# A two-layer decoder trunk: the first queries' PSUM banks emptied by ScalarE, the rotary work moved in the order, and new prices in the planner

## The chip, the cores and the metric

One Trainium2 chip, one of its eight cores. The metric is device time in microseconds of one execution. TensorE is called PE, VectorE DVE, ScalarE ACT, GpSimd POOL, and SyncE SP (here it only issues DMAs).

## The reference, cut to what matters

Two layers over 256 tokens of width 1024. Each normalises the residual stream, projects it, mixes tokens, gates the result, projects back and adds; then a gated projection of a side input is added. Layer 0 mixes by causal attention of 16 heads of 64 (with one block of 256 it is plain causal attention). Layer 1 mixes by three branches: compressed, selected and windowed keys.

```python
q = rope(rms_norm(split_heads(q, N_HEADS), q_gain), pos)   # likewise k; v is taken as it is
...
def compress(x, pe, w1, w2):
    idx = np.arange(nc)[:, None] * CMP_STRIDE + np.arange(CMP_LEN)[None, :]
    blocks = x[:, :, idx] + pe
    flat = blocks.reshape(B, G, nc, CMP_LEN * HEAD_DIM)
    return jax.nn.gelu(flat @ w1) @ w2
```

## The kernel before

**Projections.** A `Unit` is one 512-column slice of a projection. Its weights come in four groups (`step(g)`) of 128x1024 f32, 512 KB each. A group is loaded into one of five `raw` buffers by an SP DMA, rounded to fp32r by ACT (`hi<-raw`), and DVE takes the rest (`lo<-raw,hi`); the `raw` buffer is free again only when `lo` is done. The activations are split likewise (`ah`, `al`). A group then takes 12 matmuls of 512 columns: two 128-row tiles by two halves of the tokens by three products (`hi,ah`, `hi,al`, `lo,ah`). Matmuls into one bank keep their order, so a late `lo` stops all that follow on that bank. The result stands in two PSUM banks with the tag `mm`, of which there are four.

**Layer 0, first half of the heads** (`moba_half(0)`). The queries' unit `uq0` is read together with x itself; then come the keys' unit (groups called k0 to k3 here) and the values' (v0 to v3). `rope` takes the banks of the queries or the keys: ACT squares them into `tmp`, DVE sums the squares (`ssq`), makes `r` from them and from `e2`, POOL raises `r` to the power -1/2 (`r_q`, `r_k`, 128x16), and DVE multiplies the banks by the tables of cosines and sines times gain (`tq`, `tk`, made by `tables` from `cst` and `gmoba`), adds, and for keys multiplies by `r_k`. For queries DVE makes `nr_q` from `r_q`. PE then transposes `q` and `k` for the attention (`moba_attn`). After the values comes the queries' unit of the second half of the heads (uq1), which needs two of the four banks.

**Layer 1.** In `KC` the compressed branch's input `cc` is spread into windows with the position table added: 16 DVE `tensor_tensor` of 128x120 (`big<-big,pe`), whose source advances 16 elements at a time; `W(g)` multiplies the windows by the first compression weights.

**The order.** Nothing runs as it is written: `Plan.record` collects all operations, and `schedule` gives each engine a fixed order. It always takes the operation that can start first by its own prices, and of equals the one recorded first. So a step that is recorded earlier has the higher rank. Engines run their list in order, so an operation that the planner thought ready holds up everything behind it. The prices that matter: a power on POOL of n elements per partition is 900 + 130n ns (`cost`); a DMA moves 225 bytes/ns up to 6 us and 340 after (`RATE`, used in `schedule`); a DVE `tensor_tensor` is 65 + 1.04n ns. `hold` keeps DMAs back until a given operation has started: `gnsa`, `pe` and `w2`, which layer 1 needs, are held until the values' first load of the second half.

In `moba_half(0)` the recorded order is k0, k1, constants, norm, tables, rope of q, k2, k3, masks, rope of k, v0 to v3.

Of the kernel before, what the change touches and what calls it, by code (L numbers as in the profile page):

```python
# [7 lines left out]
F32 = mybir.dt.float32  # L8
F32R = mybir.dt.float32r
AF = mybir.ActivationFunctionType  # L10
OP = mybir.AluOpType
AX = mybir.AxisListType

P = 128
# [2 lines left out]
KT = 8  # L17
HD = 64
EPS = 1e-6
SWITCH = 150.0  # L20
NRAW, NHI, NLO, NPT, NA = 5, 5, 5, 9, 9
WARM = 15
ORDER = ("vw KE vs VS KT QE0 0A 0S1 0S0 VW 0T0 0S3 0T1 kc 0S2 1A 0T3 0T2 KC 1S0 1T0 q1.0 1S2 W0 q1.1 q1.2 1S3 "
         "0V 1T2 q1.3 W1 1S1 W2 1T3 W3 QE1 2A WE 2S2 0c 2S0 1c 1T1 1V 2T0 0b 2T2 2c 2S1 1b 2B 3A 3c 2T1 2S3 "
         "3S1 2T3 2V 3S0 3T1 3T0 3B 3S3 3S2 3T2 3T3 3V")

CST, CST_N = {}, 0
for _k, _n in (("ident", 128), ("cos", 128), ("sin", 128), ("mask", 384), ("cmask", 32), ("valid", 2), ("rmask", 4),
# [5 lines left out]
class View:  # L34
# [30 lines left out]
    def elems(self):  # L65
        n = 1
        for _, c in self.ap.ap[1:]:
            n *= c
        return n


class Tile_:
# [4 lines left out]
class Plan:  # L77
# [77 lines left out]
    def cost(self, op, views, first):  # L155
        n = first.elems() if isinstance(first, View) else 0
        e, m = op.engine, op.method
        if e == "sync":
            v = first if isinstance(first, View) else op.args[1]
            return v.elems() * 4 * v.ap.ap[0][1]  # L160
        if e == "tensor":
            k, c = op.args[1].ap.ap[0][1], op.args[1].ap.ap[1][1]
            op.mode = tuple(128 if x > 64 else 64 if x > 32 else 32 for x in (k, c))
            if m == "transpose":
                return 109.2
            if op.args[1].ap.dtype == mybir.dt.bfloat16:
                return 2.5 + n / 1.2
            if op.args[1].ap.dtype == F32R:
                return (n + 32) / 2.4 if n > 128 else 110

            return 2 * max(54.6 if op.mode == (128, 64) else 109.2, 2 * n / 2.4 / (2 if op.mode == (128, 64) else 1))
        if e == "gpsimd":
            if op.kwargs.get("op") == OP.pow:
                return 900 + 130.0 * n
            return 100 + 2.3 * n
        psum = any(self.tags[v.tile.tag]["psum"] for v in views)
        rows = first.ap.ap[0][1]
        half = 110 if rows in (60, 64) and (any(v.box()[0] != first.box()[0] for v in views)
                                            or psum and first.ap.dtype == F32R and e == "vector") else 0
        if e == "scalar":  # L180
            if m == "dma_start":
                return first.elems() * 4 * first.ap.ap[0][1]
            if first.tile.tag == "early":
                return 1500.0
            c = (60 if psum else 100) + 0.833 * max(n, op.args[1].elems())
            return half + c + 93 * sum(isinstance(op.kwargs.get(k), View) for k in ("scale", "bias", "accum_out"))
        if m == "tensor_tensor_reduce":
            return 130 + 1.04 * n
        if m == "reciprocal":
            return 65 + 6.9 * n  # L190
        if m == "tensor_reduce":
            return 65 + 1.04 * op.args[1].elems()
        two = len([v for v in views if v.elems() > 2 and v is not first]) > 1
        if not psum and not two and m in ("tensor_copy", "tensor_scalar"):
            return 70 + half + 0.52 * n + 60 * any(isinstance(x, View) and x.elems() == 1 for x in op.args[2:])
        return 65 + half + 1.04 * n + (65 if m == "scalar_tensor_tensor" and isinstance(op.args[2], View) else 0)

    LAT = {"PE": 200.0, "DVE": 140.0, "ACT": 160.0, "POOL": 200.0, "DMA": 100.0}
    START = {"PE": 110.0}

    ISSUE, LAG, RATE = 450.0, 2250.0, (225.0, 340.0)
    OWN = {"DVE": 127.0, "POOL": 127.0}

    def lat(self, a, b):
# [14 lines left out]
    def hold(self, since, i):  # L219

        for o in self.ops[since:]:
            o.after.append(i)

    def schedule(self):
        ops = self.ops
# [42 lines left out]
        while len(order) < n:  # L268
# [45 lines left out]
            by = "DMA" if o.method == "dma_start" else e  # L314
            if o.method == "dma_start":
                t = max(s + self.LAG, moved)
                moved = finish[i] = t + o.cost / self.RATE[t > 6000.0]
                free[e] = s + self.ISSUE
            else:
                finish[i] = free[e] = s + o.cost * (1.8 if e == "PE" and s < 5200.0 else 1.0)  # L320
# [54 lines left out]
def trunk(ctx: ExitStack, tc: tile.TileContext, a, out):  # L375
# [29 lines left out]
    def load_consts(lo, hi):  # L405
        nc.sync.dma_start(cst[:, lo:hi], a["cst"][:, lo:hi])

    def load_gains(t, lo, n):
        src = a["head_gain"]
        nc.sync.dma_start(t, bass.AP(tensor=src.tensor, offset=src.offset + 2 * HD * lo, ap=[[0, P], [1, 2 * HD * n]]))  # L410
# [159 lines left out]
            nc.copy(self.bc, ps[:, :T])  # L570


    def rope(ps, tab, nb, norm, is_q, tag, bufs):
        o = work.tile([P, 2, 512], F32, tag=tag, name=tag, bufs=bufs).rearrange("p t (h d) -> p t h d", d=HD)
        ssq = work.tile([P, 2, 8], F32, tag="ssq", name="ssq")
        for t in range(2):
            sq = tmp("hsq").rearrange("p (h d) -> p h d", d=HD)
# [28 lines left out]
    def evac_tok(o, ps, n, norm):  # L606
        for t in range(2):
            nc.scalar.activation(o[:, t], ps[t][:, :n], AF.Copy, scale=norm.rstd[:, t:t + 1])
# [116 lines left out]

    def moba_half(h):
        uq = Unit(a["moba_in"][1], False, x0).all() if h else uq0
        uk = Unit(a["moba_in"][2 + h], False, x0)
        early = 0 if h else 2
        loads = []  # L730
        for g in range(early):
            loads.append(len(nc.ops))
            uk.step(g)
        if h == 0:
            since = len(nc.ops)
            load_consts(0, 384)
            load_gains(gmoba, 0, 2)
            nc.hold(since, loads[1])

            for k in range(KT):  # L740
                n0.add(k)
            n0.finish()
            tab.append(tables("tq0", gmoba, [0]))
            tab.append(tables("tk0", gmoba, [1]))
        tq0, tk0 = tab
        q, nr = rope(uq.ps, tq0, 1, n0, True, "q", 2)
        for g in range(early, 4):
            loads.append(len(nc.ops))
            uk.step(g)
        if h == 0:  # L750
            since = len(nc.ops)
            load_consts(384, CST_N)
            nc.hold(since, loads[3])
        k, _ = rope(uk.ps, tk0, 1, n0, False, "k", 2)
        held_at.append(len(nc.ops))
        uv = Unit(a["moba_in"][4 + h], False, x0).all()
        v = work.tile([P, 2, 512], F32, tag="v", name="v")
        evac_tok(v, uv.ps, 512, n0)
        return q, nr, k, v

    def stack_moba(ps):

# [75 lines left out]
    g0 = out_proj(0, xo, n1)  # L838


    since = len(nc.ops)
    load_gains(gnsa, 2, 4)
    nc.hold(since, held_at[1])
    tq1 = tables("tq1", gnsa, [0])
    tk1 = tables("tk1", gnsa, [2, 3])
    nc.gpsimd.tensor_tensor(cosc, cosc, gnsa[:60, 1, 0], op=OP.mult)
    nc.gpsimd.tensor_tensor(sinc, sinc, gnsa[:60, 1, 1], op=OP.mult)
    since = len(nc.ops)
    pe = consts.tile([P, 2, 16], F32, name="pe")
    nc.sync.dma_start(pe, a["pe"])  # L850
    w2 = consts.tile([P, 2, 2, HD], F32, name="w2")
    nc.sync.dma_start(w2, a["w2"])
    nc.hold(since, held_at[1])


    n2 = Norm()
# [205 lines left out]
    def KC():  # L1062

        cc2 = big("cc").rearrange("p k t -> p (k t)")
        cc = [cc2[:, 0:1024], cc2[:, 1024:2048]]
        ukc = units["kc"]
        for i in range(2):
            cg = cc[i].rearrange("p (g t) -> p g t", g=4)
            cn = tmp("cn").rearrange("p (a b) -> p a b", a=2)
            nc.vector.tensor_tensor(cn, ukc.ps[i].rearrange("p (a b) -> p a b", a=2),  # L1070
                                    n2.bc[:, None, :].to_broadcast([P, 2, T]), op=OP.mult)
            for s in range(2):
                for d in range(2):

                    nc.copy(cg[d * HD:d * HD + HD, s::2, 0:T - d], cn[s * HD:s * HD + HD, :, d:T])
        kcB = consts.tile([P, 4, 32], F32, name="kcB")
        vcB = consts.tile([P, 16, HD], F32R, name="vcB")
        nc.gpsimd.memset(kcB, 0.0)
        win = []
        wins = big("win").rearrange("p k t -> p (k t)")  # L1080
        for i in range(2):
            w = wins[:, 960 * i:960 * i + 960].rearrange("p (t g n) -> p t g n", t=16, g=4)
            cg = cc[i].rearrange("p (g t) -> p g t", g=4)
            for h in range(2):
                for g in range(4):
                    src = cg[:, g, 16 * h:16 * h + 240].rearrange("p (n t u) -> p t n u", t=8, u=2)[:, :, :, 0]
                    nc.vector.tensor_tensor(w[:, 8 * h:8 * h + 8, g], src,
                                            pe[:, i, 8 * h:8 * h + 8, None].to_broadcast([P, 8, 15]), op=OP.add)
            win.append(w.rearrange("p t g n -> p t (g n)"))
        ST["win"], ST["B"], ST["y"] = win, (kcB, vcB), bank("mm", 4)  # L1090

# [201 lines left out]
```

## Time and profile before

| | us |
|---|---|
| median of 3 runs | 376.25 (375.98 to 376.69) |
| the profiled execution | 376.59 |
| its span in the trace | 374.5 |
| PE busy | 362.9 (97%) |
| DVE busy | 328.4 (88%) |
| ACT busy | 265.8 (71%) |
| POOL busy | 30.3 (8%) |

All times below are in us from the start of the span; 2.1 us of the execution lie outside it. A busy PE is not PE at its peak, since matmuls are pipelined and their ends are modelled: a matmul of 512 columns is shown as 0.39 us long, while the next one starts 0.23 us after it. In a timeline row the bracket gives the idle time of the engine just before the row, and who ended it; "x3" says that three instructions were merged into the row, and the time is then that of all.

### The profile page before, as it was taken

Reading aid. Unit: us, or ns where it says so; the run is one execution under the profiler, and the core shown is the slowest. Engines: PE = TensorE matmul, PEld = TensorE weight load, DVE = VectorE, ACT = ScalarE, POOL = GpSimd, SP = SyncE. Lnnn points to the kernel's source line nnn. Section 1 sums busy time; section 2 is a strip of 40 time slices with the busy share of each in tenths; the row PEclk is TensorE's granted clock in tenths of the full one; section 3 lists DMA queues with packets and bytes.
Section 4 is the critical chain, followed back from the end, with each engine's and each line's share of the span. In section 5 each row is a group of like instructions: output and inputs, shape, how many; then the busy total and the mean of one; then the engine's idle time right before and its main releaser. Section 6 shows DMA issues by size and latency. Waiting matters only on the chain.

```text
span 374.5 us, 7157 instructions
## 1 busy us (share of the span) xinstructions
PE 362.9 (97%) x2576; PEld 322.9 (86%) x2576; DVE 328.4 (88%) x820; ACT 265.8 (71%) x576; POOL 30.3 (8%) x21
## 2 busy tenths in 40 slices
PE   8989799999999999999999999999999999999994
PEld 6657687789999999999889999756997998999994
DVE  5877998999799895979979999998998999968864
ACT  6665478698789885755934979768966899947611
POOL 0017300330000000000013300000300000000000
PEclk9999999999999999999999999999999999999998
DMA  7976483333742445553454754054873200564012
GB/s 212 298 300 226 169 298 139 118 109 115 270 152 95 131 151 186 167 171 114 115 178 133 270 170 170 2 194 162 319 281 115 84 3 3 168 226 170 0 41 74
DMA packets 19907, 58.97 MB, mean 157 GB/s; under 512 B 2464, under 2 KB 5152, under 8 KB 19872
## 3 DMA queue, kind: packets, MB, share of 16 engines
q1 hardware_dynamic: 19584, 58.37, 45.7%
q8 instruction: 20, 0.33, 0.4%
q10 hardware_dynamic: 288, 0.15, 0.1%
q14 instruction: 15, 0.12, 0.1%
HBM read 57.46 MB, written 1.05 MB: 156 GB/s over the span
## 4 chain that ended last, share of the span: by engine, by line
PE 70%; DVE 21%; issue 4%; DMA 2%; POOL 2%; SPq 0%; ACT 0%; DVEq 0%; ACTq 0%
PE mm L353 53%; PE tr L353 10%; PE s L353 8%; DVE lo L353 4%; DVE sm L353 3%; DVE big L353 2%; DVE tmp L353 2%; POOL r_q L353 2%; DMA raw<-in_moba_in 2%; DVE k L353 1%; DVE q L353 1%; DVE ssq L353 1%; DMA gain_in<-in_gain_in 1%; DVE hl L353 1%; DVE pc L353 1%
## 5 line engine op out<-in xcount | busy, mean ns | idle before, releaser
L353 ACT ACTIVATE hi<-raw 128x1024 fp32r<-128x1024 f32 (+2 forms) x100 | 99.8, 1007 | 36.3 <-PE mm L353 16.2
L353 DVE TENSOR_TENSOR lo<-raw,hi 128x1024 fp32r<-128x1024 f32 (+2 forms) x100 | 114.2, 1156 | 5.7 <-ACT hi L353 5.3
L353 PE MATMUL mm<-ah,hi 128*128 128x256 f32 x416 | 118.6, 286 | 0.0
L353 PE MATMUL mm<-al,hi 128*128 128x256 f32 x416 | 118.4, 286 | 0.0
L353 PE MATMUL mm<-ah,lo 128*128 128x256 f32 x416 | 118.3, 286 | 0.0
L353 PEld LDWEIGHTS mm<-ah,hi 128*128 128x128 f32 x416 | 79.4, 191 | 0.8 <-issue 0.4
L353 PEld LDWEIGHTS mm<-al,hi 128*128 128x128 f32 x416 | 79.6, 192 | 0.4
L353 PEld LDWEIGHTS mm<-ah,lo 128*128 128x128 f32 x416 | 79.3, 191 | 0.5 <-issue 0.2
L353 PE MATMUL mm<-lo,ah 128*128 128x512 f32 (+2 forms) x178 | 67.7, 381 | 1.4 <-DVE lo L353 1.3
L353 PE MATMUL mm<-hi,ah 128*128 128x512 f32 (+2 forms) x178 | 67.0, 380 | 0.6 <-ACT hi L353 0.5
L353 PE MATMUL mm<-hi,al 128*128 128x512 f32 (+2 forms) x178 | 67.1, 377 | 0.0
L353 ACT ACTIVATE sm<-sm,nb 128x128 f32<-128x128 f32 (+1 forms) x96 | 42.8, 450 | 8.5 <-DVE nb L353 8.3
L353 PEld LDWEIGHTS mm<-lo,ah 128*128 128x128 f32 x178 | 34.0, 191 | 8.4 <-DVE lo L353 3.6
L353 PEld LDWEIGHTS mm<-hi,ah 128*128 128x128 f32 x178 | 33.8, 192 | 6.5 <-ACT hi L353 1.5
L353 PEld LDWEIGHTS mm<-hi,al 128*128 128x128 f32 x178 | 34.1, 192 | 5.4 <-DVE al L353 0.3
L353 DVE CUSTOM_DVE_ANT_0 sm<-s,cst,nr_q 128x128 f32<-128x128 f32 (+1 forms) x96 | 35.5, 411 | 0.3
L353 PE MATMUL tr<-cst,sm 128*128 128x128 f32 x144 | 24.8, 278 | 0.7 <-DVE sm L353 0.7
L353 ACT ACTIVATE pt<-tr 128x384 f32<-128x384 f32 x48 | 21.7, 482 | 4.8 <-PE tr L353 4.6
L353 POOL TENSOR_TENSOR r_q<-r,neg_half 128x16 f32<-128x16 f32 x5 | 18.0, 3599 | 44.0 <-DVE r L353 44.0
L353 PEld LDWEIGHTS tr<-cst,sm 128*128 128x128 f32 x144 | 17.1, 141 | 4.9 <-DVE sm L353 1.6
L353 ACT ACTIVATE tmp<-tmp 128x512 f32<-128x512 f32 (+2 forms) x21 | 11.1, 533 | 14.3 <-DVE tmp L353 14.2
L353 POOL TENSOR_TENSOR rstd<-ms,neg_half 128x2 f32<-128x2 f32 x4 | 4.0, 1006 | 209.8 <-DVE ms L353 209.8
(165 smaller groups left out, 543.6 us busy)
## 6 DMA issues: line engine op xcount, KB each, us to landing
raw<-in_moba_in SPq DMA_DIRECT2D x28, 512.0 KB, 4.6
raw<-in_nsa_in SPq DMA_DIRECT2D x24, 512.0 KB, 4.4
raw<-in_w_out SPq DMA_DIRECT2D x16, 512.0 KB, 4.5
raw<-in_ple_gate SPq DMA_DIRECT2D x16, 512.0 KB, 3.5
raw<-in_w SPq DMA_DIRECT2D x8, 512.0 KB, 3.6
raw<-in_ple_proj SPq DMA_DIRECT2D x4, 512.0 KB, 4.6
raw<-in_nsa_vs SPq DMA_DIRECT2D x4, 304.0 KB, 3.1
xT<-in_x SPq DMA_DIRECT2D x8, 128.0 KB, 4.9
```

Source lines behind the costliest of these rows:

```text
L353: getattr(getattr(self.nc, o.engine), o.method)(*[real(x) for x in o.args], **{k: real(x) for k, x in o.kwargs.items()})
```

## The change

It has four parts. In `moba_half(0)` the recorded order is now k0, k1, constants, norm, `qe`, k2, k3, masks, tables, v0, v1, rope of q, v2, v3, rope of k, evacuation of v; `qe` is new: two ACT copies of the queries' banks to SBUF, after which `rope` reads SBUF in place of PSUM. The second half keeps its order. The DMAs of `gnsa`, `pe` and `w2` are held only until v3's load of the first half. The position additions are 4 operations of 480 elements in place of 16 of 120. And the planner's prices change: a power 2300 + 130n ns, three DMA rates, a `tensor_tensor` with a wide source step 65 + 1.75n ns.

```diff
-SWITCH = 150.0
+SWITCH, POW = 150.0, 2300.0
...
+HALVES = ("k0 k1 consts norm qe k2 k3 masks tabs v0 v1 q v2 v3 k v", "q k0 k1 k2 k3 k v0 v1 v2 v3 v")
...
             if op.kwargs.get("op") == OP.pow:
-                return 900 + 130.0 * n
+                return POW + 130.0 * n
...
+        if m == "tensor_tensor" and args_step(op.args[1]) >= 16:
+            return 65 + 1.75 * n
...
-    ISSUE, LAG, RATE = 450.0, 2250.0, (225.0, 340.0)
+    ISSUE, LAG, RATE = 450.0, 2250.0, ((6000.0, 225.0), (26000.0, 280.0), (1e9, 340.0))
...
-                moved = finish[i] = t + o.cost / self.RATE[t > 6000.0]
+                moved = finish[i] = t + o.cost / next(r for end, r in self.RATE if t < end)
...
+    def rope_evac(ps, tag, bufs):
+
+        o = work.tile([P, 2, 512], F32, tag=tag, name=tag, bufs=bufs)
+        for t in range(2):
+            nc.scalar.activation(o[:, t], ps[t], AF.Copy)
+        return o
+
+    def rope(ps, tab, nb, norm, is_q, tag, bufs, o=None):
+        if o is None:
+            o = work.tile([P, 2, 512], F32, tag=tag, name=tag, bufs=bufs)
+        else:
+            ps = [o[:, t] for t in range(2)]
+        o = o.rearrange("p t (h d) -> p t h d", d=HD)
...
+        def qe():
+            o["q"] = rope_evac(uq.ps, "q", 2)
...
+        def q():
+            out["q"], out["nr"] = rope(uq.ps, tab[0], 1, n0, True, "q", 2, o.get("q"))
...
+        for step in HALVES[h].split():
+            if step in parts:
+                parts[step]()
+            else:
+                loads.append(len(nc.ops))
+                {"k": uk, "v": uv}[step[0]].step(int(step[1]))
         if h == 0:
-            since = len(nc.ops)
-            load_consts(384, CST_N)
-            nc.hold(since, loads[3])
...
+            held_at.extend(loads)
...
-    since = len(nc.ops)
-    load_gains(gnsa, 2, 4)
-    nc.hold(since, held_at[1])
+    nc.hold_on(lambda: load_gains(gnsa, 2, 4), held_at[7])
...
             for h in range(2):
-                for g in range(4):
-                    src = cg[:, g, 16 * h:16 * h + 240].rearrange("p (n t u) -> p t n u", t=8, u=2)[:, :, :, 0]
-                    nc.vector.tensor_tensor(w[:, 8 * h:8 * h + 8, g], src,
-                                            pe[:, i, 8 * h:8 * h + 8, None].to_broadcast([P, 8, 15]), op=OP.add)
+                src = cg[:, :, 16 * h:16 * h + 240].rearrange("p g (n t u) -> p t g n u", t=8, u=2)[:, :, :, :, 0]
+                nc.vector.tensor_tensor(w[:, 8 * h:8 * h + 8], src,
+                                        pe[:, i, 8 * h:8 * h + 8, None, None].to_broadcast([P, 8, 4, 15]), op=OP.add)
```

## Rows read from the trace of the kernel before

**Rows 1.** Stretches: busy (x instructions) of PE, weight loads, DVE, ACT, POOL; clock, DMA, GB/s.
```profile
18.00:25.00 7.00, 6.35 (x29) 4.67 (x29) 4.82 (x11) 4.15 (x5) 0.00 (x0) 1.00 1.00 380
25.00:36.00 11.00, 9.70 (x42) 7.18 (x42) 8.20 (x17) 6.43 (x8) 7.71 (x2) 1.00 0.58 194
36.00:47.00 11.00, 9.02 (x42) 7.06 (x41) 11.00 (x19) 5.50 (x7) 2.90 (x1) 1.00 0.50 175
47.00:57.00 10.00, 9.54 (x47) 7.66 (x45) 9.81 (x23) 7.37 (x16) 0.92 (x2) 1.00 0.88 299
57.00:70.00 13.00, 13.00 (x70) 10.61 (x71) 11.96 (x34) 10.43 (x22) 2.90 (x1) 1.00 0.23 82
...
225.00:245.00 20.00, 19.01 (x112) 15.62 (x112) 19.62 (x75) 15.33 (x49) 0.31 (x1) 1.00 0.23 80
```
**Rows 2.** Waits from 15 to 62 us: total, times, longest.
```profile
DVE nr_q L353 <- POOL r_q L353: 2.8, 1, 2.8
...
DVE tq L353 <- DMA gmoba<-in_head_gain: 2.2, 1, 2.2
...
PE tr L353 <- DVE k L353: 2.0, 2, 1.8
```
**Rows 3.** Timeline of PE: start, length, what, idle before.
```profile
22.10 0.50 PE L353 MATMUL mm<-lo,ah 128*128 128x512 f32 x1 [0.60 <-DVE lo L353]
...
28.22 0.49 PE L353 MATMUL mm<-lo,ah 128*128 128x512 f32 x1 [0.70 <-DVE lo L353]
...
43.39 0.39 PE L353 MATMUL mm<-lo,ah 128*128 128x512 f32 x1
...
46.54 0.33 PE L353 MATMUL tr<-cst,k 128*128 128x128 f32 x1 [1.78 <-DVE k L353]
```
**Rows 4.** Timeline of DVE in the same stretch.
```profile
20.62 0.29 DVE L353 TENSOR_TENSOR tq<-cst,gmoba 128x128 f32<-128x128 f32 x1 [2.18 <-DMA gmoba<-in_head_gain]
...
26.29 0.68 DVE L353 TENSOR_TENSOR q<-mm,tq 128x512 f32<-128x512 f32 x1
...
26.95 1.22 DVE L353 TENSOR_TENSOR lo<-raw,hi 128x1024 fp32r<-128x1024 f32 x1
...
29.11 3.48 DVE L353 TENSOR_TENSOR lo<-raw,hi 128x1024 fp32r<-128x1024 f32 x3
...
39.20 0.41 DVE L353 TENSOR_TENSOR tmp<-mm,tk 128x256 f32<-128x256 f32 x1
...
40.80 0.68 DVE L353 TENSOR_TENSOR k<-k,tmp 128x512 f32<-128x512 f32 x1
...
45.80 0.68 DVE L353 TENSOR_TENSOR k<-k,r_k 128x512 f32<-128x512 f32 x1
```
**Rows 5.** Timeline of ACT in the same stretch.
```profile
19.26 1.07 ACT L353 ACTIVATE tmp<-mm 128x512 f32<-128x512 f32 x2
21.92 1.06 ACT L353 ACTIVATE hi<-raw 128x1024 fp32r<-128x1024 f32 x1 [1.59 <-DMA raw<-in_moba_in]
```
**Rows 6.** Timeline of POOL's powers, and of DVE around the last of the three.
```profile
29.27 6.08 POOL L353 TENSOR_TENSOR r_q<-r,neg_half 128x16 f32<-128x16 f32 x1 [0.53 <-DVE r L353]
39.37 2.90 POOL L353 TENSOR_TENSOR r_k<-r,neg_half 128x16 f32<-128x16 f32 x1 [4.01 <-DVE r L353]
...
198.97 3.21 POOL L353 TENSOR_TENSOR r_q<-r,neg_half 128x16 f32<-128x16 f32 x1 [6.92 <-DVE r L353]
...
198.73 0.69 DVE L353 TENSOR_TENSOR q<-q,tmp 128x512 f32<-128x512 f32 x1
```
**Rows 7.** DVE groups by form, 180 to 260 us: count, busy, mean ns, idle.
```profile
L353 DVE TENSOR_TENSOR big<-big,pe 128x120 f32<-128x120 f32 x16 | 4.4, 359 | 0.0
...
L353 DVE TENSOR_TENSOR l<-l,gt 128x4 f32<-128x4 f32 x7 | 1.0, 154 | 0.0
```
**Rows 8.** Timeline at the position additions: DVE, then PE.
```profile
240.62 4.38 DVE L353 TENSOR_TENSOR big<-big,pe 128x120 f32<-128x120 f32 x16
...
244.80 1.94 PE L353 MATMUL mm<-raw,big 128*60 128x256 f32 x14 [0.78 <-DVE big L353]
```

More of the change, by code (lines that the diff above doesn't have):

```diff
@@ L69, in elems, with args_step @@
         return n
+def args_step(v):
+    return v.ap.ap[-1][0]
 class Tile_:
@@ L222, in hold, with hold_on @@
             o.after.append(i)
+    def hold_on(self, what, i):
+        since = len(self.ops)
+        what()
+        self.hold(since, i)
     def schedule(self):
@@ L570, in finish @@
             nc.copy(self.bc, ps[:, :T])
-    def rope(ps, tab, nb, norm, is_q, tag, bufs):
-        o = work.tile([P, 2, 512], F32, tag=tag, name=tag, bufs=bufs).rearrange("p t (h d) -> p t h d", d=HD)
+    def rope_evac(ps, tag, bufs):
[9 more added lines that the diff above has]
+        o = o.rearrange("p t (h d) -> p t h d", d=HD)
         ssq = work.tile([P, 2, 8], F32, tag="ssq", name="ssq")
@@ L727, in moba_half, with consts, masks, norm @@
         uq = Unit(a["moba_in"][1], False, x0).all() if h else uq0
[L728 to L734, printed above, removed]
-            since = len(nc.ops)
-            load_consts(0, 384)
-            load_gains(gmoba, 0, 2)
-            nc.hold(since, loads[1])
+        uk, uv = Unit(a["moba_in"][2 + h], False, x0), Unit(a["moba_in"][4 + h], False, x0)
+        out, o = {}, {}
+        def consts():
+            nc.hold_on(lambda: (load_consts(0, 384), load_gains(gmoba, 0, 2)), loads[1])
+        def masks():
+            nc.hold_on(lambda: load_consts(384, CST_N), loads[3])
+        def norm():
             for k in range(KT):
@@ L742, in moba_half, with tabs, ke, k @@
             n0.finish()
+        def tabs():
             tab.append(tables("tq0", gmoba, [0]))
             tab.append(tables("tk0", gmoba, [1]))
[L745 to L749, printed above, removed]
-        if h == 0:
-            since = len(nc.ops)
-            load_consts(384, CST_N)
-            nc.hold(since, loads[3])
[L754 to L759, printed above, removed]
+        def qe():
+            o["q"] = rope_evac(uq.ps, "q", 2)
+        def ke():
+            o["k"] = rope_evac(uk.ps, "k", 2)
+        def q():
+            out["q"], out["nr"] = rope(uq.ps, tab[0], 1, n0, True, "q", 2, o.get("q"))
+        def k():
+            out["k"] = rope(uk.ps, tab[1], 1, n0, False, "k", 2, o.get("k"))[0]
+        def v():
+            out["v"] = work.tile([P, 2, 512], F32, tag="v", name="v")
+            evac_tok(out["v"], uv.ps, 512, n0)
+        loads = []
+        parts = dict(consts=consts, masks=masks, norm=norm, tabs=tabs, qe=qe, ke=ke, q=q, k=k, v=v)
+        for step in HALVES[h].split():
[4 more added lines that the diff above has]
+                {"k": uk, "v": uv}[step[0]].step(int(step[1]))
+        if h == 0:
+            held_at.extend(loads)
+        return out["q"], out["nr"], out["k"], out["v"]
     def stack_moba(ps):
@@ L838, in trunk @@
     g0 = out_proj(0, xo, n1)
-    since = len(nc.ops)
-    load_gains(gnsa, 2, 4)
-    nc.hold(since, held_at[1])
+    nc.hold_on(lambda: load_gains(gnsa, 2, 4), held_at[7])
     tq1 = tables("tq1", gnsa, [0])
@@ L847, in trunk @@
     nc.gpsimd.tensor_tensor(sinc, sinc, gnsa[:60, 1, 1], op=OP.mult)
-    since = len(nc.ops)
     pe = consts.tile([P, 2, 16], F32, name="pe")
-    nc.sync.dma_start(pe, a["pe"])
     w2 = consts.tile([P, 2, 2, HD], F32, name="w2")
-    nc.sync.dma_start(w2, a["w2"])
-    nc.hold(since, held_at[1])
+    nc.hold_on(lambda: (nc.sync.dma_start(pe, a["pe"]), nc.sync.dma_start(w2, a["w2"])), held_at[7])
     n2 = Norm()
```

## The prediction

> **What bounds the kernel now.** I read the busy time by stretches first. PE is busy 97% of the span, so time can come only from the places where it stands idle and from those where it waits in its order. The stretches [rows 1] show where: subtracting busy from length, PE is idle 0.65, 1.30, 1.98 and 0.46 us between 18 and 57 us, 4.39 together, and 0.99 between 225 and 245. From 57 us on it has no gap (13.00 of 13). DVE in the same stretches is idle 2.18, then 2.80, then nothing at all from 36 to 47, and 0.19 of 10 after that. So in the front of the kernel two engines are close to full, and DVE has lost 4.98 us before the stretch in which it is saturated.
>
> The waits name both losses [rows 2]: 2.2 us are one wait of `tq` for the DMA of `gmoba`, 2.8 us one wait of `nr_q` for POOL. Neither is work that DVE needed then; both stand in its fixed order ahead of weight splits that were ready or nearly so. PE pays for it later. Its timeline [rows 3] has it wait for `lo` at 22.10 and 28.22, and 1.78 us for the transposes of `k` at 46.54.
>
> The DVE timeline tells why [rows 4]. `tq` stands ahead of k1's `lo` and waits until 20.62. Then the whole rope of q ranks above k2's `lo`: k2 is rounded by 22.98 (21.92 + 1.06 [rows 5]), but its `lo` runs only at 26.95, after the rope's last read of a bank at 26.29. Matmuls into a bank keep their order, so PE could do no more of k2.
>
> **Part 1: the new order in the first half.** It adds two ACT copies of 128x512. ACT's own square of those banks takes 1.07 us for two [rows 5], so I price the copies at that; ACT is busy 4.15 of 7 us there [rows 1] and costs nothing. If that cover failed, k2's `hi` would be up to 1.1 us later. DVE's rope gets no cheaper: 128x512 from a bank takes 0.68 us, from SBUF (`k<-k,tmp`) also 0.68 [rows 4]. What changes is rank.
>
> PE first. k1's `hi` is ready at 19.3, when ACT goes on to the squares [rows 5], and its `lo` can end 1.2 us later, at 20.6; but that hardly matters, since k2's data land at 21.92 and its `hi` ends at 22.98: this stretch is set by DMAs (busy share 1.00 [rows 1]) and stays so. So k2 starts on PE at 23.0, its `lo` ends about 24.2 in place of 28.17, and PE waits some 0.3 us for it. From k2 to v3 are 6 groups of 12 matmuls; at 0.23 us each that is 16.4 us, and 0.3 to 0.6 us more for the norm's small matmuls. The values would end at 39.9 us. Before they ended at 43.62 (43.39 + 0.23 [rows 3]): **3.7 us**.
>
> Then DVE, since PE next needs `q` and `k` transposed or two free banks, and both hang on the rope of k, which now ranks behind v2's and v3's `lo`. From the end of k1's `lo` (20.6) DVE has to do: six `lo` at 1.16 (3.48 for three), 7.0; and then, each at its length less the 0.08 by which it overlaps the next [rows 4], four table products at 0.2 (0.29), 0.8; four sums of squares of 128x512 at 0.6 (as other operations of that size, 0.68), 2.4; for q and for k each four half-products at 0.33 (0.41) and two products and two additions at 0.6, 3.7 and 3.7; small things, estimated, 0.9. That is 18.5 us, so the keys' banks are free at 39.1 and, with 1.2 us for the products by `r_k`, k stands at 40.3 if DVE never idles. In the kernel before the same work, plus two `lo` of uq1 (2.3), ended at 46.5 (45.80 + 0.68 [rows 4]). So DVE gains 46.5 - 42.6 = 3.9 us. PE finds its banks free when it needs them and fills the rest with uq1; of the 1.98 us in front of the transposes [rows 2] some 0.4 would stay. That makes 3.7 + 1.98 - 0.4 = **5.3 us at best**.
>
> **Part 2: what holds the power.** `r_q` took 6.08 us on POOL, `r_k` with the same shape 2.90 [rows 6]. The difference of 3.18 fits DVE's work: three `lo`, each reading two SBUF tensors, ran from 29.11 to 32.6 [rows 4], and 32.45 + 2.90 is the power's end. The one at 198.97 began inside a `q<-q,tmp` that ran to about 199.3 and took 0.31 more than 2.90 [rows 6]. `r_k` began during a product that reads a bank, and took 2.90. So a power that meets DVE reading two SBUF tensors waits, through all that follow without a gap.
>
> [...]
>
> The planner now prices this power 1.4 us higher, 4.38. That covers about half of 2.80: if the power is held for 3.2 us again, `nr_q` still stalls DVE by some 1.4; if held longer, by up to 2.8 as before; if a gap lets it in at once, by nothing. I take 1.4, since DVE will be waiting for DMAs around 21 to 26 us and gaps are likely there, and 0.6 more for splits placed in a DMA's wrong gap. So the front is worth 5.3 - 1.4 - 0.6 = **3.3 us**; the ends are 1.5 (DVE's own gain, if the whole 2.8 us stall and 0.7 of new gaps for DMAs come back: 4.98 - 2.8 - 0.7) and 5.3.
>
> **Part 3: earlier DMAs.** `gnsa`, `pe` and `w2` are 400 KB and move up to about 24 us, when k2's `lo` frees the buffer for v3. SP issues three more DMAs ahead of uq1's loads; at 194 to 380 GB/s [rows 1] that delays them 1 to 2 us, and uq1 is needed some 15 us later. I price it at nothing. The masks' load stays where it was. The new DMA prices move `tq` behind what is really there first; that is in part 1 already.
>
> **Part 4: position additions.** 16 operations take 4.38 us [rows 8]. A single one of 120 elements takes 359 ns, a `tensor_tensor` of 4 elements 154 [rows 7], so an element at this stride costs 205/116 = 1.77 ns. Four operations of 480 take 154 + 476 x 1.77 = 995 ns each, less 85 of overlap with the next (359 - 4380/16), so 3.6 together: 0.75 us less. PE waited 0.78 us for them [rows 8] in a stretch where it lost 0.99 [rows 1]. The planner thought each 190 ns and now prices them as they are, so PE can be given other work. Ends: 0 (the four-dimensional read could be dearer; no row shows one) and 1.0. I take **0.8**.
>
> **Part 5: the price of all other powers.** Nine later powers are priced 1.4 us too long too, and none is known to be held. An operation behind one is then placed late, not stalled. I price this at nothing, since PE had other work throughout while a power of 2.90 us ran in 57 to 70 (13.00 of 13 [rows 1]); the bounds are -0.7 (chance of a better order) and 5.6 (below).
>
> **The sum.** 376.59 - 3.3 - 0.8 = 372.5 against the profiled execution, which lies 0.34 above the median; so **372.2** for the median. Less than 0.2% (0.75 us) of this kernel can't be told from no change.
>
> **Rivals.**
> First, the power stays locked out. q's products and the splits run on DVE without a gap, POOL gets in only when `nr_q` stalls, and DVE sets the front's gain: 1.5 + 0.8, so 374.0. [...] Against: the splits now wait for DMAs between the products, and the price covers 1.4.
> Second, the lead is given back. PE comes earlier to a DVE that is idle 0.19 of 10 us from 47 to 57 [rows 1], and the attention's DVE work holds it; only part 4 pays, by half: 375.9, the same. Against: DVE's own 4.98 us of idleness lay before 47 us, so DVE comes earlier as well, and it is idle 1.04 of 13 from 57 to 70.
> Third, slower: the powers' price in layer 1. Four powers there (three `r_q`, one of the compressed keys), each priced 1.4 us too long, put keys' and queries' products late on DVE and the scores behind them late on PE. If PE has nothing else, each costs its 1.4, 5.6 together: 372.2 + 5.6 = 377.8. It decides against the change from 4.1 + 0.75 = 4.9 us on, so nearly all four must show as idle PE. For it: DVE is busy 19.62 of 20 in 225 to 245 [rows 1]. Against: PE has projections to fill with.
> That the order does not come out as recorded (`tq` once more ahead of k1's `lo`) is possible; it would cost nothing, since k2's data set that place.
>
> **How the numbers follow.** The forecast has 0.46, with its own range 371.0 to 373.4; the locked power 0.26; the lead given back 0.11; slower 0.11; and 0.06 for a front near its best end and a better order, about 370. Faster: 0.46 + 0.26 + 0.06 = 0.78; same 0.11; slower 0.11. The range from 369.8 to 376.0 leaves out the slower rival and little else.
>
> **What the profile after would show.** Right: DVE no longer waits for `gmoba`; k2's `lo` starts within 0.3 us of its `hi`; PE reaches the end of the values near 40 us and has under 1 us of gaps before the first score; the power of `r_q` is under 6 us and `nr_q` waits under 1.5; the position additions take 3.6 us and PE does not wait for them. Wrong: DVE idle behind POOL by 2.8 or more; PE waiting for banks behind the rope of k beyond 41 us; or new PE gaps between 200 and 300 us.

## The result and the profile after

The kernel after takes **370.21 us** (median of 4 runs, 370.02 to 371.09), the one before 376.12 beside it: ratio 0.9851, 95% interval 0.9823 to 0.9879, so 4.6 to 6.7 us less. The profiled execution took 370.02 us with a span of 368.2, against 376.59 and 374.5 before. Executions more than 1.5% above the fastest of their kernel count as slow and are left out; only run 5 below has any, two of ten.

Part of the difference seems to lie in TensorE's clock. Beside the experiments the kernel before ran 38 times: the median is 375.20 us in the 16 executions with a mean granted clock of 0.996 or more, and 377.26 in the 11 at 0.988 or 0.989. The kernel after had 0.997 or more in all four. Against executions of like clock, though from other batches, it gains about 5.0 us, not 5.9; why the clock differs between executions is not shown.

The stretches of the kernel after, in the columns of [rows 1]:

```profile
18.00:25.00 7.00, 7.00 (x34) 5.77 (x33) 6.19 (x13) 4.86 (x6) 1.96 (x2) 1.00 1.01 397
25.00:36.00 11.00, 11.00 (x50) 9.13 (x49) 11.00 (x21) 7.38 (x9) 6.86 (x4) 1.00 0.86 290
36.00:47.00 11.00, 11.00 (x55) 9.12 (x55) 10.88 (x15) 8.15 (x12) 1.70 (x1) 1.00 0.53 186
47.00:57.00 10.00, 10.00 (x50) 8.13 (x49) 9.94 (x26) 8.21 (x19) 2.39 (x1) 1.00 0.83 258
...
225.00:245.00 20.00, 19.80 (x128) 14.99 (x128) 19.14 (x70) 15.19 (x51) 0.00 (x0) 1.00 0.30 108
245.00:270.00 25.00, 24.14 (x194) 20.23 (x191) 22.70 (x66) 20.60 (x49) 4.75 (x3) 1.00 0.61 222
270.00:285.00 15.00, 14.78 (x124) 12.69 (x124) 13.69 (x44) 9.83 (x23) 2.61 (x1) 1.00 0.56 198
```

PE no longer idles between 18 and 57 us, where it lost 4.39. From 225 to 245 us it is idle 0.20 in place of 0.99; but from 245 to 285 new gaps of 0.86 and 0.22 stand, where before there were none.

The timeline of DVE after, around the norm and the first rope, to be read beside [rows 4]:

```profile
17.54 0.16 DVE L366 TENSOR_SCALAR ms<-tr 128x2 f32<-128x2 f32 x1 [0.28 <-PE tr L366]
...
21.94 1.22 DVE L366 TENSOR_TENSOR lo<-raw,hi 128x1024 fp32r<-128x1024 f32 x1
23.07 0.36 DVE L366 TENSOR_SCALAR r<-ssq,e 128x8 f32<-128x8 f32 x2
23.34 0.42 DVE L366 COPY bc<-tr 128x256 f32<-128x256 f32 x1
...
28.49 0.17 DVE L366 TENSOR_SCALAR nr_q<-r_q 128x16 f32<-128x16 f32 x1
...
234.25 3.71 DVE L366 TENSOR_TENSOR big<-big,pe 128x480 f32<-128x480 f32 x4
```

`ms`, the first step after the norm's sums on PE, comes at 17.54. Before it came at 26.89:

```profile
26.89 0.15 DVE L353 TENSOR_SCALAR ms<-tr 128x2 f32<-128x2 f32 x1
```

In the kernel after k2's `lo` (21.94) follows 0.3 us after the end of its `hi` (20.56 + 1.06), and `nr_q` waits for nothing. The four additions take 3.71 us together.

The timeline of POOL after, in the front, at the landmarks used below (powers that both kernels have in the same order), and late in layer 1:

```profile
23.52 2.90 POOL L366 TENSOR_TENSOR r_q<-r,neg_half 128x16 f32<-128x16 f32 x1 [5.04 <-DVE r L366]
29.44 4.24 POOL L366 TENSOR_TENSOR cst<-cst,gnsa 60x64 f32<-60x64 f32 x2 [3.02 <-DMA gnsa<-in_head_gain]
...
157.14 0.70 POOL L366 TENSOR_TENSOR rstd<-ms,neg_half 128x2 f32<-128x2 f32 x1 [84.64 <-DVE ms L366]
...
200.46 2.90 POOL L366 TENSOR_TENSOR r_q<-r,neg_half 128x16 f32<-128x16 f32 x1 [4.62 <-DVE r L366]
...
268.40 4.21 POOL L366 TENSOR_TENSOR cs<-cs,neg_half 60x1 f32<-60x1 f32 x1 [13.20 <-DVE cs L366]
348.98 0.70 POOL L366 TENSOR_TENSOR rstd<-ms,neg_half 128x2 f32<-128x2 f32 x1 [76.36 <-DVE ms L366]
```

and the same landmarks before:

```profile
163.56 0.70 POOL L353 TENSOR_TENSOR rstd<-ms,neg_half 128x2 f32<-128x2 f32 x1 [79.51 <-DVE ms L353]
...
206.80 2.90 POOL L353 TENSOR_TENSOR r_q<-r,neg_half 128x16 f32<-128x16 f32 x1 [4.62 <-DVE r L353]
...
277.16 0.54 POOL L353 TENSOR_TENSOR cs<-cs,neg_half 60x1 f32<-60x1 f32 x1 [11.25 <-DVE cs L353]
355.23 0.70 POOL L353 TENSOR_TENSOR rstd<-ms,neg_half 128x2 f32<-128x2 f32 x1 [77.53 <-DVE ms L353]
```

`r_q` takes 2.90 us in place of 6.08 [rows 6]. The lead over the kernel before is 6.42 us at the first `rstd` shown, 6.34 at `r_q` and 6.25 at the last `rstd`. So **the whole gain is made in the front**, and from `r_q` to the last `rstd` both kernels need the same (148.52 us after, 148.43 before), with 4 additions or with 16.

Some of that lead is probably not the change's: k2's data land at 20.56 us after and at 21.92 before [rows 5], 1.36 earlier, though SP issues the same DMAs in the same order up to then. It waited 1.3 us for one of x's loads before and 0.2 after. That leaves about 5.0 of the 6.4 us for the change, and the profiled execution of the kernel before is indeed 1.4 us above that kernel's median at like clock (376.59 against 375.20). That it is chance is not shown: the old order with the old rates has the two latest starts of k2's rounding (21.92, and 21.19 in run 10), and all other kernels have 19.92 to 20.72.

### The profile page after: what moved, and what is told of

Its sections match the earlier page's. It is cut to its first block, busy times and chain, and to the rows that moved or that the text cites. A ratio compares the mean times of both kernels' runs of the same rounds, so it can differ in the third digit from the quotient of the medians.

```text
span 368.2 us, 7137 instructions
## 1 busy us (share of the span) xinstructions
PE 359.8 (98%) x2576; PEld 323.2 (88%) x2576; DVE 325.5 (88%) x803; ACT 268.1 (73%) x583; POOL 33.1 (9%) x21
## 4 chain that ended last, share of the span: by engine, by line
PE 77%; DVE 13%; ACT 3%; issue 3%; POOL 1%; DMA 1%; SPq 0%; DVEq 0%; ACTq 0%
PE mm L366 58%; PE tr L366 11%; PE s L366 8%; DVE lo L366 3%; DVE sm L366 3%; DVE tmp L366 2%; DVE q L366 1%; POOL cs L366 1%; DMA tmp<-in_moba_in 1%; DVE big L366 1%; ACT ah L366 1%; ACT sm L366 1%; ACT hl L366 1%; DVE hl L366 1%; ACT qk L366 1%
## 5 line engine op out<-in xcount | busy, mean ns | idle before, releaser
L366 PE MATMUL mm<-lo,ah 128*128 128x512 f32 (+2 forms) x178 | 66.6, 376 | 0.1
L366 POOL TENSOR_TENSOR r_q<-r,neg_half 128x16 f32<-128x16 f32 x5 | 14.8, 2963 | 81.6 <-DVE r L366 81.6
L366 POOL TENSOR_TENSOR rstd<-ms,neg_half 128x2 f32<-128x2 f32 x4 | 3.1, 772 | 205.0 <-DVE ms L366 205.0
```

Of the source, the lines that this page charges most:

```text
L366: getattr(getattr(self.nc, o.engine), o.method)(*[real(x) for x in o.args], **{k: real(x) for k, x in o.kwargs.items()})
```

## The experiments

Each run is given with its ratio to the kernel before, which ran beside it. An interval is some 0.4 to 0.9% wide, so two kernels less than about 1.5 us apart are not told apart. The first kernels undo one part of the change, the others start from the kernel before or add up parts.

**1. u_order: the old recorded order in the first half, no evacuation; all else as after.**

```diff
-HALVES = ("k0 k1 consts norm qe k2 k3 masks tabs v0 v1 q v2 v3 k v", ...
+HALVES = ("k0 k1 consts norm tabs q k2 k3 masks k v0 v1 v2 v3 v", ...
```

> The changed kernel with the first half's recorded order as before (k0 k1 constants norm tables q k2 k3 masks k v0 to v3, no evacuation by ACT); the new prices, the earlier DMAs of gnsa and the 4 position additions stay. Theory A, the order made the gain: the rope of q again ranks above k2's lo, PE gets gaps of 3 us or more between 18 and 50 us, and the time is 374.0 to 376.0. Theory B, the prices made it (the planner now knows when DMAs land and powers end): DVE waits for neither gmoba nor the power, and the time stays at 370.2 to 371.7.

Measured: 371.57 us, ratio 0.9877 [0.9833, 0.9920]: Theory B's time. By the medians about 1.4 us of the gain go, not all (the intervals overlap). The timeline of PE shows the one gap that comes back, between 18 and 37 us:

```profile
27.57 0.72 PE L366 MATMUL mm<-lo,ah 128*128 128x512 f32 x2 [1.70 <-DVE lo L366]
```

It is k2's `lo` behind the rope of q, which the prediction named as PE's loss. `r_q` takes 2.90 without the new order too.

**2. u_rate: the two old DMA rates; all else as after.**

```diff
-    ISSUE, LAG, RATE = 450.0, 2250.0, ((6000.0, 225.0), (26000.0, 280.0), (1e9, 340.0))
+    ISSUE, LAG, RATE = 450.0, 2250.0, ((6000.0, 225.0), (1e9, 340.0))
```

> The changed kernel with the planner's two old DMA rates. Theory A (order): the data set the place anyway; within 0.8 us of 370.2. Theory B (prices): tq or a weight split is placed ahead of data that have not landed, DVE waits 1.5 us or more for DMAs between 17 and 27 us and PE follows; 371.7 to 373.5. Beside it: the reading stage ended 1.2 us earlier in the changed kernel than before; if the rates did that, the queries' last matmul moves back here from about 16.8 to 17.6 us, otherwise that was the chance of a DMA.

Measured: 371.96 us, ratio 0.9881 [0.9840, 0.9923]: nearer to Theory B, though 1.8 us above the kernel after is hardly clear of noise. `tq` waits 1.25 us for `gmoba` again, and the norm and the power come late:

```profile
25.31 0.82 POOL L366 TENSOR_TENSOR rstd<-ms,neg_half 128x2 f32<-128x2 f32 x1 [24.13 <-DVE ms L366]
27.80 3.81 POOL L366 TENSOR_TENSOR r_q<-r,neg_half 128x16 f32<-128x16 f32 x1 [1.67 <-DVE r L366]
```

`rstd` came at 17.77 in the kernel after. PE is idle 0.65 us from 36 to 47 and 0.30 from 47 to 57. k2's rounding starts at 20.32 here, so it is not the new rates that brought its data earlier.

**3. u_pow: the old price of a power; all else as after.**

```diff
-SWITCH, POW = 150.0, 2300.0
+SWITCH, POW = 150.0, 900.0
```

> The changed kernel with the old price of a power (900 + 130n ns). The power of r_q ended 2.1 us before nr_q was due, so theory A expects no stall of nr_q in the front and a time within 0.7 us of 370.2. Theory B: nr_q is placed 1.4 us earlier and the power is met by reads of two SBUF tensors, so the stall of nr_q returns with 1 to 2.8 us; 371.2 to 373.0. Theory C, the longer price costs something in layer 1: faster, 368.8 to 369.8.

Measured: 370.87 us, ratio 0.9863 [0.9818, 0.9909], not told apart from the kernel after; Theory A. The power runs from 24.53 to 27.43 and `nr_q` at 27.77 doesn't wait: with the rates in place the price has nothing to cover.

**4. u_pos: 16 additions again, priced at 1.75 ns an element; all else as after.**

```diff
-                nc.vector.tensor_tensor(w[:, 8 * h:8 * h + 8], src,
+                for g in range(4):
+                    nc.vector.tensor_tensor(w[:, 8 * h:8 * h + 8, g], src,
```

> The changed kernel with 16 position additions of 120 elements again, now priced with 1.75 ns an element (275 ns each, what they take). If the fewer operations are worth the 0.8 us that was forecast: 370.8 to 371.3. If it was the right price that took PE's wait away, or if the gaps between 245 and 285 us took the gain back: 369.8 to 370.6.

Measured: 371.01 us, ratio 0.9864 [0.9826, 0.9902]. The median lies in the range that was expected if the additions are worth 0.8 us, but it is not told apart from the kernel after. The stretches decide:

```profile
225.00:245.00 20.00, 19.02 (x116) 13.94 (x115) 18.83 (x77) 14.49 (x48) 0.31 (x1) 1.00 0.24 88
245.00:270.00 25.00, 25.00 (x206) 21.15 (x205) 23.27 (x69) 22.19 (x54) 2.90 (x1) 1.00 0.66 237
270.00:285.00 15.00, 15.00 (x106) 13.24 (x106) 13.20 (x40) 8.63 (x19) 0.54 (x1) 0.89 0.66 239
```

PE's gap of 0.98 us from 225 to 245 is back, but from 245 to 285 it has none. The sum of its gaps from 225 to 285 is 0.98, against 1.28 after. The additions' wait is removed and paid again at later splits and transposes. From `r_q` to the last `rstd`, the landmarks above, the five traces with 16 additions and a full clock take 148.37 to 148.60 us (before, runs 6, 9, 10 and 11), the five with 4 take 148.52 to 148.74 (after, runs 1, 2, 3 and 8). The other four, this run's among them (149.30), had a lower clock between 270 and 302 us (0.89 from 270 to 285 in runs 4, 7 and 12; 0.96 from 270 to 285 and 0.93 from 285 to 302 in run 5) and take 149.24 to 149.50.

**5. o_order: the kernel before with the new order, the evacuation and the earlier DMAs; prices and 16 additions as before.**

```diff
+SWITCH, POW = 150.0, 900.0
+HALVES = ("k0 k1 consts norm qe k2 k3 masks tabs v0 v1 q v2 v3 k v", ...
...
+    ISSUE, LAG, RATE = 450.0, 2250.0, ((6000.0, 225.0), (1e9, 340.0))
```

> The kernel before with the new recorded order of the first half alone (ACT's evacuation and the earlier DMAs of gnsa, pe and w2 with it); the old power price, the old DMA rates, 16 additions at their old price. Undoing the order cost 1.4 us and undoing the rates 1.7, far less than the gain of 5.9. Theory D, order and rates repair the same loss, and either does most of it: 371.5 to 373.3, with DVE waiting 1 to 1.5 us for gmoba and PE idle about 1 us between 18 and 57 us. Theory E, the gain is a sum of small independent parts: then the order alone gives about 1.4 us and the time is 374.3 to 375.3.

Measured: 375.15 us (median of 8 executions, 371.31 to 376.62), ratio 0.9971 [0.9938, 1.0004]: **the order alone shows no gain that is clear of noise** (1.1 us by the ratio, -0.2 to 2.3). The time is in Theory E's range. This is the run that overturns the prediction's account. Its timeline of DVE:

```profile
24.99 0.15 DVE L364 TENSOR_SCALAR ms<-tr 128x2 f32<-128x2 f32 x1
...
31.69 1.21 DVE L364 TENSOR_TENSOR lo<-raw,hi 128x1024 fp32r<-128x1024 f32 x1
35.70 0.26 DVE L364 TENSOR_SCALAR nr_q<-r_q 128x16 f32<-128x16 f32 x1 [2.80 <-POOL r_q L364]
```

of POOL:

```profile
29.18 6.49 POOL L364 TENSOR_TENSOR r_q<-r,neg_half 128x16 f32<-128x16 f32 x1 [3.13 <-DVE r L364]
```

and of PE, at the transposes of k:

```profile
42.92 0.33 PE L364 MATMUL tr<-cst,k 128*128 128x128 f32 x1 [1.85 <-DVE k L364]
45.26 0.48 PE L364 MATMUL tr<-cst,k 128*128 128x128 f32 x1 [1.08 <-DVE k L364]
```

The norm is nearly as late as before, the power meets DVE's splits and products and is shut out until the last of them ends (31.69 + 1.21 = 32.90; 29.18 + 6.49 - 2.90 = 32.77). `nr_q` stalls DVE by 2.80, and 2.93 us are missing at the transposes of k. PE's granted clock fell in this execution:

```profile
36.00:47.00 11.00, 8.08 (x34) 6.16 (x33) 11.00 (x19) 4.76 (x8) 3.62 (x2) 0.91 0.30 108
47.00:57.00 10.00, 10.00 (x49) 8.32 (x48) 9.24 (x24) 6.41 (x15) 0.00 (x0) 0.93 0.72 243
```

In PE's timeline matmuls of 512 columns start 0.23 us apart up to 40.47 and again from 48.45 on, but 0.43 apart from 45.97 to 48.10, right behind the second of PE's two gaps. By the two stretches the fall can hide up to 1.7 us of what the order gains in this execution (0.09 x 11 + 0.07 x 10, an estimate). A second fall, 0.96 from 270 to 285 and 0.93 from 285 to 302, came while PE had no gap (busy 15.00 of 15 and 17.00 of 17). The trace is of the slowest of the eight executions. In the four with a mean clock of 0.997 or more the order alone takes 373.7 us on average (371.31 to 375.54), against 375.2 for the six of the kernel before with 0.996 or more beside them: 1.5 us, too few runs to call it shown.

**6. o_rate: the kernel before with the new DMA rates and the earlier DMAs; old order, old power price, 16 additions.**

```diff
-    ISSUE, LAG, RATE = 450.0, 2250.0, (225.0, 340.0)
+    ISSUE, LAG, RATE = 450.0, 2250.0, ((6000.0, 225.0), (26000.0, 280.0), (1e9, 340.0))
```

> The kernel before with the three new DMA rates in the planner and the earlier DMAs of gnsa, pe and w2, nothing else. Theory D: 372.0 to 373.5, tq does not wait for gmoba, and with DVE in step the power of r_q begins earlier and meets fewer reads of two SBUF tensors. Theory E: 374 to 375.3. If the power's price is needed for the front as well, nr_q stalls by over 1 us here.

Measured: 371.25 us, ratio 0.9900 [0.9870, 0.9930]: with the old order, most of the gain (3.8 us by the ratio, 2.6 to 4.9). The timeline of DVE:

```profile
17.50 0.16 DVE L364 TENSOR_SCALAR ms<-tr 128x2 f32<-128x2 f32 x1 [0.23 <-PE tr L364]
...
21.59 0.41 DVE L364 TENSOR_TENSOR tmp<-mm,tq 128x256 f32<-128x256 f32 x1
...
25.85 0.16 DVE L364 TENSOR_SCALAR nr_q<-r_q 128x16 f32<-128x16 f32 x1
```

and of POOL:

```profile
21.76 2.91 POOL L364 TENSOR_TENSOR r_q<-r,neg_half 128x16 f32<-128x16 f32 x1 [3.31 <-DVE r L364]
```

and of PE, at the norm's sums, followed by the same in the kernel before:

```profile
16.96 0.50 PE L364 MATMUL tr<-ones,sqacc 128*128 128x2 f32 x4
```
```profile
24.50 0.50 PE L353 MATMUL tr<-ones,sqacc 128*128 128x2 f32 x4
```

The norm is 7.5 us earlier than with the order alone (`ms` at 17.50 and 24.99), the power starts during a product that reads a bank, and is done before `nr_q` needs it. The earlier DMAs are in run 5 too, so it is the rates that move the norm. The time is below Theory D's range and far from the 374 to 375.3 of Theory E: the gain is not a sum of small independent parts.

**7. o_prices: as after, with the old order and 16 additions** (edits 1 and 4 together).

> The changed kernel without its new order and without the four-operation additions: old order, 16 additions, but all prices new (power, DMA rates, 1.75 ns an element) and the earlier DMAs. Theory D: 371.5 to 373.0, PE idle 1.5 to 2.0 us in 25 to 36 behind k2's lo and nowhere else before 90. Theory E: 373.5 to 375.

Measured: 371.84 us, ratio 0.9906 [0.9884, 0.9929]; PE idle 0.45 us from 18 to 25 and 1.25 from 25 to 36: Theory D. The power's price adds nothing measurable to the rates (371.25 in run 6).

**8. u_qe: as after, but rope reads the banks; the new order stays.**

```diff
-HALVES = ("k0 k1 consts norm qe k2 k3 masks tabs v0 v1 q v2 v3 k v", ...
+HALVES = ("k0 k1 consts norm k2 k3 masks tabs v0 v1 q v2 v3 k v", ...
```

> The changed kernel without ACT's evacuation of the queries' banks: the order stays, rope reads PSUM, so the banks come free only when the rope behind v1's lo has read them. If the evacuation is what lets the rope rank so low: PE waits for banks before v0, some 1 us or more between 25 and 36 us, 371.5 to 373. If it is not needed: v0's first matmul comes at about 28.3 us and the rope's last read of a bank before that, so 369.9 to 370.7.

Measured: 369.59 us, ratio 0.9851 [0.9825, 0.9878]. PE has no gap from 11 to 90 us here either: the evacuation, the first part of the change by name, is not needed.

The first eight leave two accounts. Either the late norm itself holds the front, or it holds it through the power that DVE locks out (6.08 us before, 6.49 in run 5). Three more runs part them.

**9, 10. o_copy and b_copy: run 5 and the kernel before, without the power of r_q in layer 0's two halves; this leaves out q's normalisation.**

```diff
-        nc.gpsimd.tensor_tensor(r..., r0..., neg_half, op=OP.pow)
+        if is_q and norm is n0:
+            nc.scalar.activation(r..., r0..., AF.Copy)
+        else:
+            nc.gpsimd.tensor_tensor(r..., r0..., neg_half, op=OP.pow)
```

> The new order alone (with its evacuation and earlier DMAs, old prices, 16 additions) had no gain: 375.51 us, and its trace had nr_q wait 2.80 us for a power of 6.49 us, and PE wait 2.92 us ahead of the transposes of k. Here the power of r_q is left out of both halves of the first layer: r_q is an ACT copy of its input, so q is not normalised and the output is not the reference's. Theory A (the old DMA rates cost through the locked power): without the power nr_q waits under 0.5 us, PE's 2.9 us of waiting in 36 to 47 us go with it, and the time falls by 2.5 to 3.2, to 372.3 to 373.0. Theory B (the late small matmuls of the norm themselves hold the front, and the stall of nr_q only takes what DVE would wait for elsewhere): r stays at 28.7 us, the time falls by under 0.8, to 374.7 or more.

> The kernel before, with r_q as an ACT copy of its input in both halves of the first layer (no normalisation of q, so the output is not the reference's); apart from nr_q, which moves ahead of two splits, its order on DVE in the front stays. Theory A (the locked power is what the front of the kernel before pays for): DVE wins its 2.8 us of waiting, PE's wait of 1.98 us ahead of the transposes of k goes, and the time falls by 2.0 to 2.8, to 373.3 to 374.1. Theory B (PE's loss is set by k2's late lo and the late values): the time falls by under 0.8, to 375.3 or more.

Measured: o_copy 372.53 us, ratio 0.9900 [0.9872, 0.9928]; b_copy 372.70, ratio 0.9908 [0.9879, 0.9937]. **Theory A, twice**, though b_copy falls by a little more than the 2.0 to 2.8 it said (3.5 us by the ratio, 2.4 to 4.6). The power of the second half can have no part in it, since PE has no gap while that one runs, between 57 and 70 us [rows 1]. In b_copy the norm is as late as before and `tq` still waits for `gmoba`, so neither of them by itself is what cost these 3.5 us. The stretches of b_copy:

```profile
18.00:25.00 7.00, 6.59 (x30) 5.17 (x30) 5.10 (x13) 4.04 (x6) 0.00 (x0) 1.00 0.98 393
25.00:36.00 11.00, 9.71 (x42) 7.22 (x41) 11.00 (x22) 7.29 (x10) 1.83 (x2) 1.00 0.54 185
36.00:47.00 11.00, 11.00 (x52) 9.08 (x51) 10.88 (x17) 6.85 (x10) 2.70 (x1) 1.00 0.72 252
```

`ms` in its timeline of DVE:

```profile
26.20 0.15 DVE L353 TENSOR_SCALAR ms<-tr 128x2 f32<-128x2 f32 x1
```

and the first landmark in its timeline of POOL:

```profile
160.00 0.69 POOL L353 TENSOR_TENSOR rstd<-ms,neg_half 128x2 f32<-128x2 f32 x1 [79.53 <-DVE ms L353]
```

PE's gap of 1.98 us in front of the transposes [rows 1] is gone, the 1.29 from 25 to 36 stay, and the lead at `rstd` is 3.56, 0.73 of it from earlier data (k2's rounding starts at 21.19). In o_copy PE has 0.25 us of gaps from 18 to 57.

**11. o_pow: run 5 with the new price of the power; old rates, 16 additions.**

```diff
-SWITCH, POW = 150.0, 900.0
+SWITCH, POW = 150.0, 2300.0
```

> The new order alone plus the new price of the power, 2300 in place of 900; DMA rates old, 16 additions. It differs from the kernel after by rates and additions only. Theory A (with the old rates the planner meets a locked power, and the price then pays as cover): nr_q is placed later and waits under 1 us, r_q may take up to 6 us, the time falls from the 375.5 of the order alone to 372.0 to 373.0. Theory B (only the rates free the front; what the run with old rates won over the order alone came from elsewhere): nr_q still waits 2 us or more, time 374.5 or more.

Measured: 371.66 us, ratio 0.9888 [0.9851, 0.9925]: Theory A, a little better than it said. The timeline of DVE:

```profile
26.64 1.23 DVE L364 TENSOR_TENSOR lo<-raw,hi 128x1024 fp32r<-128x1024 f32 x1
27.79 0.42 DVE L364 COPY bc<-tr 128x256 f32<-128x256 f32 x1
...
32.04 0.27 DVE L364 TENSOR_SCALAR nr_q<-r_q 128x16 f32<-128x16 f32 x1
```

and of POOL:

```profile
26.66 3.98 POOL L364 TENSOR_TENSOR r_q<-r,neg_half 128x16 f32<-128x16 f32 x1 [1.67 <-DVE r L364]
```

The power is held for one split and gets in when the copy from a bank starts (26.66 + 3.98 - 2.90 = 27.74), and `nr_q` is now placed behind one more split, so it doesn't wait.

**12. u_best: as after, without the evacuation and with the power at 900** (edits 8 and 3).

> The kernel after without ACT's evacuation of the first queries (rope reads its banks again) and with the old price of the power, 900; the new order, the new DMA rates, the earlier DMAs and the 4 additions stay. Theory A (the DMA rates place the norm's small matmuls so early that the power of r_q runs unlocked; evacuation and power price are then not needed): r_q starts near 22 us and takes 2.90, PE shows no gap from 11 to 70 us, the time is 369.0 to 370.3, as the kernel after or up to 1 us better. Theory B (the price is what protects the power once it is there): r_q over 4 us or nr_q waiting over 1 us, time 371 or more.

Measured: 369.62 us, ratio 0.9836 [0.9802, 0.9871]; `r_q` from 22.34, 2.91 us, and no gap of PE from 11 to 70. Theory A. Neither this nor run 8 is measurably faster than the kernel after; both do without an edit or two of it.

## Why the prediction held, and where it did not

The time (forecast 372.2, range 369.8 to 376.0) and the sign held; the account of where the gain comes from did not.

- **What is late next.** Right in the large: PE's losses between 18 and 57 us were what there was to win, and they are gone. These 4.39 us and the 1.36 of earlier data are 0.7 less than the lead of 6.42; where the rest comes from was not traced. The values end at 39.45 us. The prediction has 39.9, from data 1.36 later, but its own terms give more: 23.0, 0.3, 16.6 (72 x 0.23, not 16.4) and 0.3 to 0.6 are 40.2 to 40.5. The transposes of k come at 40.60 and 41.17 without a wait.
- **Part 1, "5.3 us at best".** Right as a size: 6.4 at the landmark, about 5.0 without the earlier data. That is partly luck, for the cause was wrong ("What changes is rank"), and rank alone (run 5) gave 0.3% [-0.04%, 0.6%]. Where the power is free, rank is worth about 1.4 us by medians (run 1 against the kernel after); the intervals overlap, but the gap of 1.70 us is in the trace.
- **Part 2, the locked power: the term that was mis-sized.** 1.4 us of stall and 0.6 of wrong gaps were taken off; both measured nothing in the kernel after (2.90 us, `nr_q` without a wait). The rows had shown the lock, and it was right that it decides: in the kernel before it cost 3.5 us (run 10), its 2.80 of DVE time and perhaps more (2.4 to 4.6). What the prediction missed is that the change frees the power twice over, by the norm's earlier place and by the price. Rates without the price and the order, and the price with the order but without the rates, give nearly the same (runs 6 and 11: 371.25 and 371.66), so their gains don't add.
- **Part 3, "The new DMA prices move `tq` behind what is really there first; that is in part 1 already": the step that failed.** With the earlier DMAs, and with nothing else of the change, they gave 3.8 us (run 6). They move not only `tq` but the norm's sums on PE (16.96 us in place of 24.50), and with them `r`, and so the power: `r_q` starts at 21.76 in place of 29.27 and takes 2.91. The prediction never asked when `r` itself comes, only what the power meets. A planner that is told that data come sooner than they do finds other work for PE and leaves the norm; that is argued from `schedule`, while the shift itself is seen in run 6.
- **Part 4, 0.8 us.** The operations were right (981 to 1002 ns where 995 was worked out, 3.71 us together where 3.6 was; PE doesn't wait for them), the gain is not there: 148.52 against 148.43 us between the landmarks. PE now waits 0.7 us for splits and 0.6 for three transposes between 225 and 302 us, of which 0.2 was there before. New gaps between 200 and 300 us were one of the prediction's own signs of being wrong.
- **Part 5, nothing.** Held, within the 1.5 us that can be told (run 3).
- **The rivals.** The locked power is what happens with the order alone, and its price fits: DVE's own 1.5 us were forecast, and run 5 gave 1.1 by its ratio (-0.2 to 2.3). The lead was not given back, 6.25 of 6.42 us last to the end. The price of the powers in layer 1 left no mark: with the old price (run 3) the stretch from `r_q` to the last `rstd` takes 148.74 us, against 148.52 after.

In sum, the forecast's 4.1 us, with the 2.0 that were taken off for nothing and without the 0.8 that didn't come, make 5.3 us for the change; with 1.4 of earlier data that is 6.7, against 6.57 between the two profiled executions, and 5.0 was measured at like clock. So the total came near for reasons that are in part not the forecast's. Open stay the shares of rates and order within 1.5 us, the earlier DMAs by themselves (not tried), and whether the order alone would show more at full clock.

## What to carry to other kernels

When an operation of an engine beside the critical ones takes longer than others of its shape, take it out once and time the kernel: that shows whether the stall behind it (2.8 us here) reaches the end of the kernel (3.5 us, 2.4 to 4.6). Where an order comes out of a planner, its wrong prices cost through operations far from the one that is priced wrongly, so ask of each price which chain moves as a whole. And two edits that remove the same stall must not be added.

## What the runs showed of the hardware

How long the POOL power `r_q` took in the front went with what DVE did at that moment. It took 2.90 us where DVE was reading a bank when it started (2.90 or 2.91 in the kernel after and runs 3, 6 and 12), and 6.49, 3.98 and 3.81 (runs 5, 11 and 2) where it met operations with two SBUF tensors. The evacuation makes rope's products read SBUF; that this lengthens the power is not shown: run 5 has the longest of all, but only 0.41 us longer than the kernel before without an evacuation (6.08), and no run has the new order and a late power without it. A small operation took longer too: `cs` (60x1) took 4.21 us after against 0.54 before. DVE's timeline after shows what it met:

```profile
268.45 1.21 DVE L366 TENSOR_TENSOR lo<-raw,hi 128x1024 fp32r<-128x1024 f32 x1
269.59 0.21 DVE L366 TENSOR_TENSOR c<-c,cst 60x64 f32<-60x64 f32 x1
269.72 1.21 DVE L366 TENSOR_TENSOR lo<-raw,hi 128x1024 fp32r<-128x1024 f32 x1
270.86 0.21 DVE L366 TENSOR_TENSOR c<-c,csq 60x64 f32<-60x64 f32 x1
271.00 1.21 DVE L366 TENSOR_TENSOR lo<-raw,hi 128x1024 fp32r<-128x1024 f32 x1
272.65 0.28 DVE L366 TENSOR_SCALAR c<-c,cs 60x128 f32<-60x128 f32 x1 [0.44 <-POOL cs L366]
```

DVE has no gap until 272.21, and `cs` ends at 272.61, 0.40 later. Two DVE operations with two SBUF tensors, each in the middle of a power, took no longer in return: the split at 24.01 in the kernel after its usual 1.22 us, during `r_q`, and `k<-k,tmp` at 40.80 in the kernel before its usual 0.68, during `r_k` [rows 4, 6].

The reading at the start is not steady. In runs 5 and 10 SP issues the loads from 13.5 to 15.6 us within 0.1 us of each other, but k2's rounding starts at 20.20 in one and at 21.19 in the other; over all traces it starts between 19.92 (run 11) and 21.92 us (before). A difference of this size between two traces need not belong to an edit.
